# Turning the up projections of a SwiGLU layer round: tokens stationary, weights streamed

## The chip, the cores and the metric

The kernel runs on one core of one Trainium2 chip. The metric is the time of one execution on the device in microseconds (us). The profile is that of one execution; engines are named as in it: PE (matrix products), PEld (its loads of the stationary operand), DVE, ACT, POOL, and SP, which here only issues transfers.

## What is computed

One layer of a conditioned decoder trunk on 256 tokens of width 2048, all in float32: a gated feed forward, a mixer (attention heads beside a state-space part), and a second gated feed forward, each with its own shift, scale and gate from a conditioning vector and a layer norm behind it. The change touches the two feed forwards:

```python
D_MODEL = 2048
SEQ = 256
D_FF = 5632

def _modulate(h, shift, scale):
    return h * (1 + scale[:, None, :]) + shift[:, None, :]

def _swiglu(u, w1, w3, w2):
    return (jax.nn.silu(u @ w1) * (u @ w3)) @ w2

mod = (silu(c) @ w_cond[i] + b_cond[i]).reshape(B, N_SUBLAYERS, 3, D_MODEL)
u = _modulate(x, mod[:, 0, 0], mod[:, 0, 1])
h = _swiglu(u, ffn1_w1[i], ffn1_w3[i], ffn1_w2[i])
x = _layer_norm(DEEPNORM_ALPHA * x + FFN_RES_WEIGHT * (1 + mod[:, 0, 2])[:, None, :] * h, ...)
```

## The kernel before

All weights come as a stream of pieces of 128 x 1024 float32 (512 KB). A `Job` (line 110) holds one piece's source, its products (`mm`), and what is issued behind it (`post`). `Stream.run` (line 660) issues the jobs in order. For every piece SP loads `raw`, ACT rounds it to `hi` (fp32r, line 647), and DVE makes `lo = raw - hi` (line 657); activations are held as such a pair too. One product then takes three: hi with hi, hi with the activation's low part, lo with the activation's high part. `AHEAD = 4` (line 34) pieces are split ahead of PE; `RAW` and `RW` (lines 33, 59) set how many are being loaded, three or four.

The order on each engine is that of the program text. `stream.later(n, f)` puts `f` behind the n-th following piece; a post step stands on its engine ahead of the split of the piece four further on. The calls of DVE and PE pass through wrappers, and so the profile shows line 106 for all of them; ACT's own lines are kept.

**Up, before.** `form_a` (line 710) and the products in `mk_ko` (line 883) have the weights stationary, 128 x 128 at a time, and stream 256 tokens of `U`, the modulated input with its columns on the partitions (`Uh`, `Ul`). What comes out has the feed forward's columns on the partitions, as the down projection needs it. `up_post` (line 931) takes Silu on ACT (`sg`), multiplies on DVE (`h`), and splits the product into `Hh` (ACT, line 943) and `Hl` (DVE), one step per following piece.

**Down.** `mk_down` (line 960) uses `form_b` (line 731): 128 tokens of `H` stationary, 512 columns of weights streamed, both halves of the tokens one after the other, two tiles of k per piece, 12 products a piece.

**Order of a feed forward** (`ffn`, line 879). It has 44 tiles of 128 columns, treated as `PIECES` of 16, 16 and 12 tiles: up, then down, for each. The first 20 tiles are done in passes over ranges of k, because `U` gets ready bit by bit: four passes of four k-tiles in the first feed forward, two of eight in the second. Partial sums of 16 tiles go to `kosum` (copied by ACT in the first pass, added by DVE in later ones); four tiles (`KEEP`) stay in four of the eight PSUM banks. A feed forward has 264 pieces, 176 up and 88 down.

**Beside it.** Conditioning: 288 pieces of `w_cond` are loaded into `gv` and multiplied and summed by DVE (`gv_step`, line 215); a quarter of a shift and scale takes 16 of them, and `modulate` (line 280) then makes `U`. In the first feed forward's passes each piece has its share of these steps (`GA`, line 46). Afterwards `drain` (line 322) deals out conditioning steps and the preparation of the state-space matrices (`bg5`): it issues as long as DVE's estimated time is under PE's plus `LIM[0]` = 2.6. `Meter` (line 83) adds up both estimates, here for PE:

```python
n = x.shape[-1]
self.t += n / 2350.0 if name == "matmul" and a[1].dtype == F32R else max(n, 100) / 1170.0
```

Before the second feed forward the normalised rows are transposed in pairs of tiles (`turn`, line 835). Two of these steps stand in `mid` and are issued between the products of the first piece, ahead of its k-tiles 2 and 4 (`between`, line 705); the mixer's start does the same. The residual and the norm close each part (`last_block`, line 739).

Of the kernel before, what the change touches and what calls it, by code (L numbers as in the profile page):

```python
# [63 lines left out]
class Later:  # L64
    """Records the calls of an engine with their approximate costs, to be issued one by one."""
# [17 lines left out]
class Meter:  # L83
    """Passes the calls of an engine on and adds up their approximate costs in microseconds."""
# [6 lines left out]
    def __getattr__(self, name):  # L91
        f = getattr(self.engine, name)

        def call(*a, **k):
            x = k["out"] if "out" in k else a[0]
            if name in ("matmul", "transpose"):
                n = x.shape[-1]
                self.t += n / 2350.0 if name == "matmul" and a[1].dtype == F32R else max(n, 100) / 1170.0
            else:
                if name in ("tensor_reduce", "bn_stats"):  # L100
                    x = a[1]
                n = 1
                for d in x.shape[1:]:
                    n *= d
                self.t += 0.07 + n / (1920.0 if name in self.FAST else 960.0)
            return f(*a, **k)  # L106
        return call


class Job:  # L110
    """One piece of weights [128, 1024] and what is done with it."""
# [6 lines left out]
def tile_layer(tc, A, out):  # L118
    nc = tc.nc
    V, S, PE, SP, GP = Meter(nc.vector), nc.scalar, Meter(nc.tensor), nc.sync, nc.gpsimd  # L120
    with ExitStack() as ctx:
# [23 lines left out]
        def cells(t):  # L145
            """[128, 32] pieces of a slab"""
# [48 lines left out]
        # a unit is a quarter of the columns of a shift and of its scale ("p"), or half of a gate's ("g")  # L195
# [35 lines left out]
        def finish(u, acc, j0, j1):  # L231
            """gain and offset of some tiles of columns from the two halves of their sums"""
# [47 lines left out]
        def modulate(blk, q, j0=0, j1=4):  # L280
            """the second operand of the products, for some of a quarter of the columns"""
# [40 lines left out]
        def drain():  # L322
            """issues background work as VectorE has room for it"""
# [83 lines left out]
        def cmul(V, ore, oim, ar, ai, br, bi, t1, t2, conj_im=False):  # L407
            """o = a*b; with conj_im, ai and oim hold the negated imaginary parts."""
# [11 lines left out]
        def s5_prep():  # L420
# [31 lines left out]
            # powers 1 to 4 of the discretised state matrix, in the place of what is no longer used  # L452
# [15 lines left out]
            # per quarter of the groups: [inputs 512 | temporaries 256 | -c_im 128 | . | W 1024 | C 1024 | est 1024]  # L468
# [22 lines left out]
            def quarter_ops(q):  # L491
                g0 = 8 * q

                def go():
# [7 lines left out]
                    def powers(z, x, p, s0, s1):  # L502
                        """z[r] = x * p, for several powers; s0 and s1 follow from the sign of the imaginary part"""
# [201 lines left out]
        def between(k):  # L705
            """what is due before the products of k-tile k"""
            if k in mid:
                mid.pop(k)()

        def form_a(p, hi, lo, UH, UL, k0, first, last):  # L710
            """p [128 columns, 256 tokens] += weights^T u^T, eight k-tiles"""
# [7 lines left out]
        def form_b1(p, hi, lo, AH, AL, k0, t, first, last, c0=0, c1=512):  # L719
            """p [128 tokens, columns c0 to c1] += a weights, two k-tiles"""  # L720
# [18 lines left out]
        def last_block(B, ops, db, sub):  # L739
            """the last block of columns of a sub-layer: its last pieces go to one half of the tokens first"""  # L740
# [28 lines left out]
        def newton(o, sd, hv, q):  # L769
            """o = 1 / sqrt(v) from sd, its root, and hv = -v / 2"""  # L770
# [8 lines left out]
        def residual(t, db, p, c0=0, c1=512):  # L779
            """r = gate * p + z on one block of columns, and its statistics"""  # L780
# [8 lines left out]
        def ln_token(sub, t):  # L789
            """statistics and normalisation of one half of the tokens"""  # L790
# [36 lines left out]
        def load_affine(sub, new, h):  # L827
            """half of the columns of a norm's gain and bias"""
# [6 lines left out]
        def turn(ks, then):  # L835
            """pairs of column tiles of the normalised rows, transposed; what comes of each goes to then"""
# [23 lines left out]
        def affine(t, q, last):  # L860
            """x = normalised * g + b, in place"""
# [17 lines left out]
        def ffn(w13, w2, blk, passes, tiles, kept):  # L879
# [3 lines left out]
            def mk_ko(i, f, m):  # L883
                """a range of k for one tile of columns; both products at once when m is None"""
                k0, k1 = passes[i]
                keep = f in kept
                first = i == 0 or not keep
                last = i == len(passes) - 1 or not keep
                n = k1 - k0

                def mm(hi, lo):
                    ms = (0, 1) if m is None else (m,)
                    if first and ms[0] == 0:
                        B["ko", f] = psum()
                    for a, x in enumerate(ms):
                        p = B["ko", f][:, x * 256:(x + 1) * 256]
                        for k in range(n):
                            between(k0 + k)
                            w = hi[:, (a * n + k) * 128:(a * n + k + 1) * 128]
                            PE.matmul(p, w, kx(st["U"][0], k0 + k), start=first and k == 0 and x == 0, stop=False,  # L900
                                      skip_group_check=True)
                            PE.matmul(p, w, kx(st["U"][1], k0 + k), start=False, stop=False, skip_group_check=True)
                    for a, x in enumerate(ms):
                        p = B["ko", f][:, x * 256:(x + 1) * 256]
                        for k in range(n):
                            PE.matmul(p, lo[:, (a * n + k) * 128:(a * n + k + 1) * 128], kx(st["U"][0], k0 + k),
                                      start=False, stop=last and k == n - 1, skip_group_check=True)

                def post():
                    if keep:  # L910
                        if i == len(passes) - 1 and f < 16:
                            up_post(B["ko", f], f)
                        return
                    p = B["ko", f]
                    n = [x for x in range(tiles) if x not in kept].index(f)
                    if i == 0 and n % 4 == 0:
                        B["sum", n // 4] = pslab("kosum") if n // 4 < 2 else slab("kosum")
                    a = B["sum", n // 4][:, n % 4 * 512:(n % 4 + 1) * 512]
                    if i == 0:
                        S.copy(a, p)  # L920
                    else:
                        V.tensor_tensor(a, p, a, op=ALU.add)
                    if i == len(passes) - 1:
                        stream.later(1, lambda: up_post(a, f))
                if m is None:
                    src = w13[f, :, :, k0 * 128:k1 * 128].rearrange("m p x -> p m x")
                else:
                    src = w13[f, m, :, k0 * 128:k1 * 128]
                return Job(mm, src, post if m != 0 else None)

            def up_post(p, slot):
                if slot == 0:
                    st["H"] = pairs("H")
                s, h = w1([128, T], "sg"), w1([128, T], "h")
                hh, hl = kx(st["H"][0], slot), kx(st["H"][1], slot)
                S.activation(s, p[:, 0:256], AF.Silu)  # L936

                def mul():
                    V.tensor_tensor(h, s, p[:, 256:512], op=ALU.mult)
                    stream.later(1, hi)  # L940

                def hi():
                    S.copy(hh, h)  # L943
                    stream.later(1, lo)

                def lo():
                    V.tensor_tensor(hl, h, hh.bitcast(F32), op=ALU.subtract)
                stream.later(1, mul)

            def mk_up(ft, m, h, slot):  # L950
                def mm(hi, lo):
                    if m == 0 and h == 0:
                        B["ps"] = psum()
                    form_a(B["ps"][:, m * 256:(m + 1) * 256], hi, lo, *st["U"], 8 * h, h == 0, h == 1)

                def post():
                    up_post(B["ps"], slot)
                return Job(mm, halves(w13[ft, m], h), post if m and h else None)

            def mk_down(pi, db, c, nch, f):  # L960
# [17 lines left out]
                src = halves(w2[db, f // 4], f // 2 % 2)  # L978
# [6 lines left out]
            def load_z(db):  # L985
                """the gate and, for the first of the two, the input on a block of columns"""
# [31 lines left out]
            for i, (k0, k1) in enumerate(passes):  # L1018
                n = len(jobs)
                for f in range(tiles):  # L1020
                    jobs += [mk_ko(i, f, m) for m in ((None,) if k1 - k0 == 4 else (0, 1))]
                jobs[n].pre.append(lambda k0=k0, k1=k1: [gv_until("ready", blk, q) for q in range(k0 // 4, k1 // 4)])
            for pi, (f0, nf) in enumerate(PIECES):
                n = len(jobs)
                for s in range(max(0, min(tiles - f0, nf)), nf):
                    for m in range(2):
                        for h in range(2):
                            jobs.append(mk_up(f0 + s, m, h, s))
                if pi == 1:
                    for s in range(tiles - f0):  # L1030
# [554 lines left out]
```

## Time and profile before

| | |
|---|---|
| median of three runs | 1949.61 us (1946.49 to 1951.14) |
| span of the profiled execution | 1946.0 us; it has no other time of its own, and the three runs lie 0.5 to 5.1 us above it |
| mean granted clock of PE | 0.994 |
| first feed forward, passes over k | 33 to 272 us |
| its remainder | 272 to 810 us |
| mixer | 810 to 1179 us |
| second feed forward, passes over k | 1179 to 1412 us |
| its remainder | 1412 to 1946 us |

The stages are cut where PE's timeline passes from one kind of products to the next. A product's duration in the profile contains its way through the array, and products overlap; what a product costs in a stream is the step from its start to that of the next. "Busy" time of PE is the time in which any product is under way. In the views by stretches a product that lies across an edge is counted on both sides.

### The profile page before, as it was taken

The page shows a single profiled execution, that of the slowest core. Times are in us where ns is not written, and L with a number is a line of the kernel's source. Part 1 is how long each engine was busy: PE and PEld are TensorE (multiplying, and loading weights), DVE is VectorE, ACT ScalarE, POOL GpSimd, SP SyncE. Part 2 cuts the span into 40 slices and gives each one's busy share as a digit, 9 for nine tenths or more (in the row PEclk, how much of TensorE's full clock was granted, in tenths as well). Part 3 has the DMA queues.
Part 4 walks back from the last instruction along what each step waited for, and adds up shares of the span by engine and source line. Part 5 has one row for each costly group of instructions (what it writes and reads, how often), then busy time and mean ns, then how long its engine had stood idle before and what let it go on. Part 6 is the DMA issues. An engine that isn't in the chain of part 4 may idle for free.

```text
span 1946.0 us, 33739 instructions
## 1 busy us (share of the span) xinstructions
PE 1883.6 (97%) x13342; PEld 1763.9 (91%) x13342; DVE 1499.4 (77%) x2373; ACT 896.2 (46%) x1289; POOL 64.5 (3%) x119
## 2 busy tenths in 40 slices
PE   3999999999999999899999999999999999999997
PEld 2999997999889998799998888999988999899986
DVE  5899889787877888897998997888866544544468
ACT  2544544545445443443447635444444444334442
POOL 0000000000000000101210000000000000000000
PEclk9999999999999999999999999999999999999999
DMA  8999757899898889799988796998876555555573
GB/s 300 364 358 337 237 197 282 293 335 317 303 338 301 308 301 330 253 341 309 310 282 316 263 328 233 331 333 268 288 283 247 185 185 183 194 191 179 185 246 121
DMA packets 162064, 532.88 MB, mean 274 GB/s; under 512 B 21825, under 2 KB 23281, under 8 KB 160753
## 3 DMA queue, kind: packets, MB, share of 16 engines
q1 hardware_dynamic: 147330, 495.31, 72.3%
q0 software_dynamic: 6512, 23.89, 3.6%
q10 hardware_dynamic: 8064, 11.54, 1.7%
q8 instruction: 104, 1.70, 0.4%
q14 instruction: 54, 0.44, 0.1%
HBM read 513.34 MB, written 17.33 MB: 273 GB/s over the span
## 4 chain that ended last, share of the span: by engine, by line
PE 89%; DVE 6%; DMA 3%; ACT 1%; issue 1%; POOL 0%; SPq 0%; DVEq 0%; ACTq 0%; POOLq 0%
PE ps L106 89%; DVE lo L106 2%; DVE Y L106 1%; DMA gv<-in_w_cond_dram 1%; DVE gv L106 1%; DVE cells L106 1%; DMA raw<-in_f1w_dram 1%; DMA U<-sD 1%; DMA X<-in_x_dram 0%; DVE st L106 0%; ACT hi L647 0%; DVE r L106 0%; DMA sD<-sT 0%; ACT Y L818 0%; DMA sc<-in_c_dram 0%
## 5 line engine op out<-in xcount | busy, mean ns | idle before, releaser
L106 DVE TENSOR_TENSOR lo<-raw,hi 128x1024 fp32r<-128x1024 f32 x630 | 767.7, 1223 | 366.4 <-ACT hi L647 360.2
L647 ACT CAST hi<-raw 128x1024 fp32r<-128x1024 f32 x630 | 659.2, 1050 | 610.9 <-PE ps L106 422.3
L106 PE MATMUL ps<-Uh,hi 128*128 128x256 f32 x3200 | 793.4, 285 | 29.8 <-ACT hi L647 21.0
L106 PE MATMUL ps<-Ul,hi 128*128 128x256 f32 x3200 | 789.7, 284 | 0.3
L106 PEld LDWEIGHTS ps<-Uh,hi 128*128 128x128 f32 x3200 | 616.6, 193 | 37.3 <-ACT hi L647 23.0
L106 PEld LDWEIGHTS ps<-Ul,hi 128*128 128x128 f32 x3200 | 616.6, 193 | 2.2 <-DVE Ul L106 1.9
L106 PE MATMUL ps<-Uh,lo 128*128 128x256 f32 x3200 | 449.9, 283 | 0.0
L106 PEld LDWEIGHTS ps<-Uh,lo 128*128 128x128 f32 x3200 | 413.6, 192 | 0.0
L106 DVE SCALAR_TENSOR_TENSOR gv<-gv,sc 128x1024 f32<-128x1024 f32 x288 | 351.0, 1220 | 16.0 <-DMA gv<-in_w_cond_dram 8.9
L106 PE MATMUL ps<-hi,Hh 128*128 128x512 f32 (+1 forms) x716 | 274.4, 384 | 0.0
L106 PE MATMUL ps<-hi,Hl 128*128 128x512 f32 (+1 forms) x716 | 274.1, 384 | 0.0
L106 PE MATMUL ps<-lo,Hh 128*128 128x512 f32 (+1 forms) x716 | 217.6, 385 | 5.7 <-DVE lo L106 5.5
L106 PEld LDWEIGHTS ps<-lo,Hh 128*128 128x128 f32 x716 | 133.0, 189 | 34.4 <-DVE lo L106 8.2
L106 PEld LDWEIGHTS ps<-hi,Hh 128*128 128x128 f32 x716 | 134.8, 188 | 26.7 <-issue 0.4
L106 PEld LDWEIGHTS ps<-hi,Hl 128*128 128x128 f32 x716 | 134.9, 188 | 26.4
L936 ACT ACTIVATE sg<-ps 128x256 f32<-128x256 f32 x56 | 21.5, 384 | 116.0 <-PE ps L106 116.0
L106 DVE TENSOR_TENSOR kosum<-ps,kosum 128x512 f32<-128x512 f32 x64 | 44.2, 690 | 23.1 <-PE ps L106 23.1
L943 ACT CAST Hh<-h 128x256 fp32r<-128x256 f32 x88 | 35.4, 402 | 43.1 <-DVE h L106 43.0
L106 PE MATMUL ps<-hi,Ah 128*128 128x512 f32 (+1 forms) x144 | 52.1, 367 | 0.0
L106 PE MATMUL ps<-hi,Al 128*128 128x512 f32 (+1 forms) x144 | 52.0, 366 | 0.0
L106 PE MATMUL ps<-lo,Ah 128*128 128x512 f32 (+1 forms) x144 | 40.9, 366 | 0.0
L920 ACT COPY kosum<-ps 128x512 f32<-128x512 f32 x32 | 18.8, 586 | 45.2 <-PE ps L106 45.1
(211 smaller groups left out, 1182.4 us busy)
## 6 DMA issues: line engine op xcount, KB each, us to landing
gv<-in_w_cond_dram SPq DMA_DIRECT2D x288, 512.0 KB, 6.7
raw<-in_f1w_dram SPq DMA_DIRECT2D x264, 512.0 KB, 5.6
raw<-in_f2w_dram SPq DMA_DIRECT2D x264, 512.0 KB, 4.4
raw<-in_win_a_dram SPq DMA_DIRECT2D x48, 512.0 KB, 5.6
raw<-in_wout_dram SPq DMA_DIRECT2D x32, 512.0 KB, 5.5
s5m<-scrB POOLq DMA_DIRECT2D x8, 1024.0 KB, 7.9
raw<-in_win_v_dram SPq DMA_DIRECT2D x16, 512.0 KB, 4.5
scrB<-s5f ACTq DMA_DIRECT2D x8, 640.0 KB, 9.4
```

Of the source, the lines that this page charges most:

```text
L106: return f(*a, **k)
L647: S.copy(hi, raw)
L920: S.copy(a, p)
L936: S.activation(s, p[:, 0:256], AF.Silu)
L943: S.copy(hh, h)
```

## The change

The up projections take the form of the down projections. `form_b` is used in `mk_ko` and `mk_up` with `U` stationary, and w1 or w3 streamed 512 columns wide. One block is four tiles of columns; its w1 products (m = 0) come first, then those of w3 (m = 1), eight pieces each, or as many as the pass has. Only the first block of a feed forward takes w1 and w3 by turns. The result has tokens on the partitions, in two PSUM banks of 512 columns for each of w1 and w3. `gated` takes Silu behind the last w1 piece, `up_post` multiplies in place behind the last w3 piece, and two and three pieces later four 128 x 128 transposes each bring two tiles into `H`'s layout in one PSUM bank, from which ACT and DVE make `Hh` and `Hl`. The number and size of pieces stay. The weights are laid out by `blocks`, so that a piece is 128 rows of 1024 words in one run; in the first feed forward's passes it was two runs of 512 words per row.

The estimate of PE's time per product changes with it, and at the second feed forward's start the two turns come behind pieces 0 and 1, not between the first piece's products.

```diff
-                self.t += n / 2350.0 if name == "matmul" and a[1].dtype == F32R else max(n, 100) / 1170.0
+                self.t += (n + 32) / 2400.0 if name == "matmul" and a[1].dtype == F32R else max(n, 100) / 1170.0
...
-            def mk_ko(i, f, m):
+            def mk_ko(i, b, m, kp):
...
                 def mm(hi, lo):
...
+                    if first and 2 * kp == k0:
+                        B["ko", b, m] = [psum(), psum()]
+                    form_b(B["ko", b, m], hi, lo, *st["U"], 2 * kp, first and 2 * kp == k0, last and 2 * kp + 2 == k1)
...
+                    a = [B["sum", b][:, (2 * m + t) * 512:(2 * m + t + 1) * 512] for t in range(2)]
+                    for t in range(2):
+                        if i == 0:
+                            S.copy(a[t], ps[t])
+                        else:
+                            V.tensor_tensor(a[t], ps[t], a[t], op=ALU.add)
                     if i == len(passes) - 1:
-                        stream.later(1, lambda: up_post(a, f))
...
+                        if m == 0:
+                            B["a", b] = a
+                            stream.later(1, lambda: gated(a, a))
+                        else:
+                            s = B.pop(("a", b))
+                            stream.later(1, lambda: up_post(s, a, 4 * b))
+                return Job(mm, halves(w13[b, m, kp // 2], kp % 2), post if 2 * kp + 2 == k1 else None)
+
+            def gated(ps, s=None):
+                s = s or [w2([128, 512], "sg") for _ in range(2)]
+                for t in range(2):
+                    S.activation(s[t], ps[t], AF.Silu)
+                return s
+
+            def up_post(s, ps, slot):
                 if slot == 0:
                     st["H"] = pairs("H")
...
+                for t in range(2):
+                    V.tensor_tensor(s[t], s[t], ps[t], op=ALU.mult)
+
+                def turned(i):
+                    p = psum()
+                    for j in range(2):
+                        for t in range(2):
+                            PE.transpose(p[:, j * T + t * 128:j * T + t * 128 + 128],
+                                         s[t][:, (2 * i + j) * 128:(2 * i + j + 1) * 128], ident)
+                    hh, hl = (kx(x, slot + 2 * i, 0, 2 * T) for x in st["H"])
+                    S.copy(hh, p)
+                    V.tensor_tensor(hl, p, hh.bitcast(F32), op=ALU.subtract)
+                stream.later(2, lambda: turned(0))
+                stream.later(3, lambda: turned(1))
+
+            def mk_up(b, m, kp, slot):
                 def mm(hi, lo):
...
+                    if kp == 0:
+                        B["ps", m] = [psum(), psum()]
+                    form_b(B["ps", m], hi, lo, *st["U"], 2 * kp, kp == 0, kp == 7)
                 def post():
...
+                    if m == 0:
+                        B["s"] = gated(B.pop(("ps", 0)))
+                    else:
+                        up_post(B.pop("s"), B.pop(("ps", 1)), slot)
...
-                for f in range(tiles):
-                    jobs += [mk_ko(i, f, m) for m in ((None,) if k1 - k0 == 4 else (0, 1))]
+                for b in range(tiles // 4):
+                    kps = range(k0 // 2, k1 // 2)
+                    if (i, b) == (0, 0):
+                        jobs += [mk_ko(i, b, m, kp) for kp in kps for m in range(2)]
+                    else:
+                        jobs += [mk_ko(i, b, m, kp) for m in range(2) for kp in kps]
...
-        mid[2] = lambda: turn((2,), turn_mod(6))
-        mid[4] = lambda: turn((3,), turn_mod(6))
+        stream.later(0, lambda: turn((2,), turn_mod(6)))
+        stream.later(1, lambda: turn((3,), turn_mod(6)))
...
-        o[f"f{i}w13"] = np.stack(up, 1).reshape(NF, 2, 128, D)
+        o[f"f{i}w13"] = np.stack([blocks(a[f"ffn{i}_w{j}"][0]) for j in (1, 3)], 1)
```

## What the change was predicted to do

> **What bounds the kernel now.** I read the page first: the share of each engine, then the chain of work that ended last.
>
> ```profile
> PE 1883.6 (97%) x13342; PEld 1763.9 (91%) x13342; DVE 1499.4 (77%) x2373; ACT 896.2 (46%) x1289; POOL 64.5 (3%) x119
> ...
> PE 89%; DVE 6%; DMA 3%; ACT 1%; issue 1%; POOL 0%; SPq 0%; DVEq 0%; ACTq 0%; POOLq 0%
> PE ps L106 89%; DVE lo L106 2%; DVE Y L106 1%; DMA gv<-in_w_cond_dram 1%; DVE gv L106 1%; DVE cells L106 1%; DMA raw<-in_f1w_dram 1%; DMA U<-sD 1%; DMA X<-in_x_dram 0%; DVE st L106 0%; ACT hi L647 0%; DVE r L106 0%; DMA sD<-sT 0%; ACT Y L818 0%; DMA sc<-in_c_dram 0%
> ```
>
> Nine tenths of the chain are products on PE. An average can hide stages with another limit, so next come busy times by stretches of 50 us (columns: stretch, then PE, PEld, DVE, ACT, POOL, granted clock, DMA share, GB/s).
>
> ```profile
> 50.00:100.00 50.00, 50.00 (x419) 50.00 (x418) 43.82 (x79) 27.87 (x38) 0.00 (x0) 1.00 1.00 368
> 100.00:150.00 50.00, 50.00 (x419) 50.00 (x418) 48.68 (x67) 18.60 (x18) 0.00 (x0) 1.00 0.97 352
> ...
> 300.00:350.00 50.00, 49.28 (x215) 39.77 (x214) 48.92 (x110) 20.78 (x22) 0.00 (x0) 1.00 0.83 299
> ...
> 1550.00:1600.00 50.00, 50.00 (x419) 50.00 (x418) 25.06 (x27) 21.20 (x28) 0.00 (x0) 1.00 0.52 179
> ```
>
> PE has work all the time, at the full granted clock, in all four. But in the first feed forward DVE (48.68 of 50) and the DMA engines (1.00) are nearly full beside it, while in the second DVE and DMA are half idle. So the second will pay out what PE saves, and the first only as far as DVE and DMA can follow.
>
> **What one piece of weights costs PE.** Both forms run in this kernel already: the up projections stream 256 tokens, the down projections 512 columns. PE's timeline in order of time gives the true step from start to start:
>
> ```profile
> 1450.67 0.39 PE L106 MATMUL ps<-hi,Hh 128*128 128x512 f32 x1
> ...
> 1464.28 0.39 PE L106 MATMUL ps<-hi,Hh 128*128 128x512 f32 x1
> ...
> 1560.04 0.28 PE L106 MATMUL ps<-Uh,hi 128*128 128x256 f32 x1
> ...
> 1562.92 0.28 PE L106 MATMUL ps<-Uh,hi 128*128 128x256 f32 x1
> ```
>
> The second pair is one piece: 24 products in 2.88 us, 0.120 each. Between the first pair lie 60 products: 13.61 us, 0.2268 each. Twice the columns cost less than twice the time: the two rows give about 0.013 us per product and 0.107 per 256 columns. A turned piece is 12 products of 512: 2.722 us, so **0.158 us less per piece**.
>
> The DMA issues count the pieces:
>
> ```profile
> raw<-in_f1w_dram SPq DMA_DIRECT2D x264, 512.0 KB, 5.6
> raw<-in_f2w_dram SPq DMA_DIRECT2D x264, 512.0 KB, 4.4
> ```
>
> Each feed forward has 264, of which 88 go down (44 tiles in twos, four blocks); 176 go up, 352 in both. 352 x 0.158 = **55.6 us saved on PE**. The operands are as in the down form (stationary fp32r activations, moving fp32r weights), so I take its step.
>
> **What is added on PE.** Per block of 512 columns the gated product is transposed in two groups of four; 11 blocks in each of two feed forwards make 44 groups, 176 transposes. The S5 preparation shows eight inside a stream of products:
>
> ```profile
> 631.74 1.12 PE L106 MATMUL ps<-Uh,lo 128*128 128x256 f32 x8
> 632.70 1.04 PE L106 MATMUL ps<-ident,s5w 128*128 128x128 f32 x8
> 633.66 0.67 PE L106 MATMUL ps<-s5f,s5w 128*32 128x128 f32 x16
> ...
> L106 PE MATMUL ps<-ident,s5w 128*128 128x128 f32 x64 | 8.3, 272 | 0.0
> ```
>
> From the first to what follows them: 0.96 us for eight, 0.12 each, though one lasts 272 ns: they overlap. 44 x 0.48 = **21.1 us added**. The Trainium skill, "TensorE: Matmul & The Clock Gate", Part 4: PE-mode transpose, has a transpose at about 275 ns in one kernel's context; if that were the step, 176 would cost an estimated 48 us and eat nearly the whole saving. The trace agrees with it as a duration (272), not as a step.
>
> Net: 55.6 - 21.1 = 34.5 us, half in each feed forward.
>
> **What is added off PE.** Per four tiles, four multiplications and four subtractions of 256 become two and two of 512, four Silu and four casts on ACT two and two.
>
> ```profile
> L106 DVE TENSOR_TENSOR kosum<-ps,kosum 128x512 f32<-128x512 f32 x64 | 44.2, 690 | 23.1 <-PE ps L106 23.1
> L106 DVE TENSOR_TENSOR Hl<-h,Hh 128x256 fp32r<-128x256 f32 x88 | 36.8, 420 | 0.0
> ```
>
> On DVE 8 x 0.42 = 3.36 us become 4 x 0.69 = 2.76: lighter. I give it nothing, since DVE isn't the end where it has room. The order gets tighter, though. The copy of the turned block (ACT) now waits for PE's transposes, the subtraction (DVE) for that copy; behind them queue the split of the piece four ahead (hi, then lo) and, on SP, the load that follows that lo. From PE's product to the subtraction go 0.48 for the transposes and about 0.6 for the copy: DVE may stand about 1.1 us, 44 times. Cover: three pieces are split ahead, 3 x 2.72 = 8.2 us. Without it, at most 44 x 1.1 = 48 us. In the passes over k, PSUM is emptied two banks at a time with four to rotate: DVE must be done two pieces (5.4 us) after a pair, where it had three; also covered unless DVE lags by over 4 us. SP issues the same number of pieces of the same size.
>
> **The first feed forward's passes.** DVE there does lo, a conditioning step and a sum per piece:
>
> ```profile
> 104.60 0.68 DVE L106 TENSOR_TENSOR kosum<-ps,kosum 128x512 f32<-128x512 f32 x1
> ...
> 117.85 0.69 DVE L106 TENSOR_TENSOR kosum<-ps,kosum 128x512 f32<-128x512 f32 x1
> ...
> 151.22 0.17 DVE L106 SCALAR_TENSOR_TENSOR gs<-acc 128x4 f32<-128x4 f32 x1
> ...
> 155.65 1.23 DVE L106 TENSOR_TENSOR lo<-raw,hi 128x1024 fp32r<-128x1024 f32 x1 [0.53 <-ACT hi L647]
> ```
>
> Five pieces took DVE 13.25 us with no idle between. PE needs 5 x 2.88 = 14.4 now and 5 x 2.722 = 13.6 then: DVE still fits, by 0.36 us instead of 1.15. But each new quarter of k holds DVE 4.4 us with its modulation (151.22 to 155.65), and at 0.36 per five pieces it hardly catches up in the twenty of a pass. I take 1 us lost, between 0 and 40 pieces x 0.158 = 6.3.
>
> **Its remainder.** There the background (S5 preparation, conditioning) is dealt out by the program's estimate of PE's time. That estimate was 24 x 256/2350 = 2.614 us per piece, under the true 2.88; it becomes 12 x 544/2400 = 2.720, the true time. So DVE may be given 0.106 us more per piece and has no hidden margin left. 184 pieces lie here: at most 19.5 us. Where DVE was full, PE did stop:
>
> ```profile
> 300.00:320.00 20.00, 19.23 (x62) 1.00 0.75 271
> 320.00:340.00 20.00, 19.73 (x35) 1.00 0.89 326
> ...
> 420.00:440.00 20.00, 19.93 (x30) 1.00 0.88 299
> ...
> 500.00:520.00 20.00, 19.68 (x29) 1.00 0.75 267
> ...
> 766.38 1.22 PE L106 MATMUL ps<-lo,Hh 128*128 128x512 f32 x2 [2.77 <-DVE lo L106]
> ```
>
> (The middle rows are DVE's busy time in stretches of 20 us.) Some 50 pieces lie in such full stretches: 50 x 0.106 = 5.3. I take **5 us lost**, between 0 and 19.5.
>
> **The starts.** Before the second feed forward the first piece needed all of k 0 to 7, with two turns in its middle:
>
> ```profile
> 1179.02 0.58 PE L106 MATMUL ps<-Uh,hi 128*128 128x256 f32 x1 [0.91 <-DVE Uh L106]
> ...
> 1185.93 0.28 PE L106 MATMUL ps<-Uh,hi 128*128 128x256 f32 x1
> ...
> 1180.00:1200.00 20.00, 19.78 (x150) 0.94 0.65 212
> ```
>
> 6.91 us for 2.88 of work. The new first piece needs k 0 and 1 alone, and the turns come behind pieces 0 and 1: their eight transposes, and on ACT and DVE the modulation of two k each, still ahead of the splits of pieces 4 and 5, and wanted only by pieces 4 and 6. 6.91 - 2.88 - 0.96 (the transposes stay) = 3.1 at most; the granted clock of 0.94 over 20 us (the last row) is 1.2 us that stays too. I take **2 gained**, between 0 and 3.1. At the very start the opposite:
>
> ```profile
> 39.90 0.58 PE L106 MATMUL ps<-Uh,hi 128*128 128x256 f32 x1 [5.17 <-ACT Uh L293]
> ...
> 40.23 4.62 DVE L106 TENSOR_TENSOR lo<-raw,hi 128x1024 fp32r<-128x1024 f32 x4
> ```
>
> The first piece can now begin earlier with k 0 and 1, but its fifth product is of lo, which DVE makes last, at about 41.4, where the old piece went on at 39.90 with hi. I take 0.5 lost, between 0 and 1.5.
>
> **Sum.** -55.6 + 21.1 + 1 + 5 - 2 + 0.5 = -30.0 us. The span is 1946.0, to 1916.0; the median of the runs is 1949.61, 3.6 above it, and I keep that distance: **1919.6 us**.
>
> **Rivals.**
> *DVE becomes the end throughout the first feed forward.* For: 48.68 and 48.92 of 50. Against, after the passes:
>
> ```profile
> 272.30:810.40 538.10, 532.71 (x3592) 487.41 (x3591) 450.36 (x797) 248.10 (x370) 17.98 (x33) 1.00 0.85 303
> ```
>
> DVE is busy 450 of 538 us, 84%, and at most 19.5 us more could be dealt out early. The first half then gives nothing: 17.2 + 2 - 0.5 = 18.7 saved, 1930.9. Chance 0.16.
>
> *DMA.* Between 60 and 100 us:
>
> ```profile
> raw<-in_f1w_dram SPq DMA_DIRECT2D x14, 512.0 KB, 7.5
> gv<-in_w_cond_dram SPq DMA_DIRECT2D x14, 512.0 KB, 7.5
> xT<-in_xT_dram SPq DMA_DIRECT2D x1, 512.0 KB, 8.4
> ```
>
> 29 pieces in 40 us. The new pace asks 40/2.722 x 1.9 + 1 = 28.9: just what was moved. If it can't be held, the 60 + 40 pieces of the passes that share the queue with conditioning gain nothing: 15.8 less, 1935.4. Chance 0.05.
>
> *The transposes don't overlap,* at 272 ns each: 47.9 instead of 21.1, 1946.4, no change. For: groups of four lie between two waits. Against: the 0.96. Chance 0.02.
>
> *The width saves nothing:* 512 columns of these weights at twice 0.120; the point is 0.2268 + 30/(352 x 12) = 0.234. All 55.6 gone: 1975.2. Against: 60 products in a row. Chance 0.02. The Trainium skill, same page, section Back-to-back issue gap, has the gap at N/2.4 + 2.5 ns, which is 109 and 216: it would save an estimated 11 us before the transposes, and the change would lose. The measured 120 and 227 speak against that rule.
>
> *Slower, by PE's wait at the turns* of the first feed forward: a full DVE delivers the product late, and PE, which runs in order, stands at the transposes. Two pieces (5.4 us) cover it; it decides above 30/22 = 1.4 us per turn. At the 2.77 us that PE waited for a late lo, 22 x 2.77 = 61: 1980.6. Chance 0.03.
>
> **Chances and range.** The forecast, 1911 to 1926, has 0.66; better than that 0.06 (no loss in the first feed forward is 1913.6; a cheaper turn goes below). 1908 to 1935 leaves out about 0.03 below and 0.14 above. A change under 0.2% (3.9 us) can't be told from none. Faster 0.93, same 0.02, slower 0.05.
>
> **What would show it.** In the changed profile: 12 products per up piece at 0.227; eleven blocks x 2 with groups of four transposes whose next product starts 0.48 later; in the second feed forward PE without idle and about 19 us shorter; in the first, DVE near full between 100 and 350 us and a few waits of PE for lo. Wrong would be a PE idle at transposes (the turn's rival), passes that still take 2.88 per piece, or a step above 0.23.

## The result, and the profile after

The changed kernel takes 1925.01 us (median of four runs, 1920.76 to 1926.62); the kernel before, timed with it, 1948.05 (1946.22 to 1951.14). The ratio is 0.9877, with a 95% interval of 0.986 to 0.9894: 23 us faster, where 30 were forecast. The profiled execution took 1923.86 us with a span of 1921.6.

The page of the changed kernel, its span, its engines and its chain by engine:

```profile
span 1921.6 us, 25394 instructions
...
PE 1853.3 (96%) x9294; PEld 1559.2 (81%) x9294; DVE 1492.8 (78%) x2285; ACT 884.1 (46%) x1201; POOL 65.5 (3%) x119
...
PE 83%; DVE 9%; DMA 4%; ACT 2%; issue 2%; POOL 0%; SPq 0%; DVEq 0%; ACTq 0%
```

PE is busy 30 us less, DVE and ACT hardly changed. PE is still the bound, but its part of the chain falls from 89% to 83% and DVE's rises from 6% to 9%.

Where the time went is read by stages. The edges are the first product of a stage on PE's timeline: passes of the first feed forward, its remainder, mixer, the first two pieces of the second feed forward, and its rest. Before:

```profile
33.09:272.34 239.25, 234.08 (x1921) 233.61 (x1922) 208.33 (x323) 114.83 (x151) 4.01 (x4) 1.00 0.86 309
272.34:810.48 538.14, 532.75 (x3593) 487.45 (x3592) 450.36 (x797) 248.14 (x370) 18.06 (x33) 1.00 0.85 303
810.48:1179.02 368.54, 356.55 (x2485) 328.88 (x2483) 328.66 (x587) 193.69 (x354) 37.67 (x68) 0.99 0.87 301
1179.02:1188.81 9.79, 9.57 (x57) 8.52 (x57) 8.81 (x16) 8.28 (x14) 0.00 (x0) 0.83 0.27 92
1188.81:1946.00 757.19, 743.45 (x5288) 702.95 (x5286) 485.52 (x612) 323.62 (x391) 3.20 (x6) 0.99 0.66 231
```

After (columns as in the prediction: stretch, length, PE, PEld, DVE, ACT, POOL, granted clock, DMA share, GB/s; the last row is a detail of the second):

```profile
32.03:264.63 232.60, 225.87 (x992) 184.21 (x993) 206.40 (x306) 109.94 (x133) 4.02 (x4) 1.00 0.88 319
264.63:796.27 531.64, 525.15 (x2497) 432.64 (x2496) 448.13 (x770) 247.48 (x343) 19.25 (x34) 1.00 0.87 306
796.27:1166.14 369.87, 357.54 (x2485) 329.85 (x2484) 327.80 (x587) 193.37 (x354) 37.44 (x67) 0.99 0.88 300
1166.14:1181.30 15.16, 11.23 (x33) 7.80 (x33) 8.87 (x13) 6.90 (x11) 0.00 (x0) 0.66 0.26 83
1181.30:1921.60 740.30, 726.33 (x3289) 602.20 (x3287) 484.60 (x570) 318.77 (x350) 3.20 (x6) 0.99 0.69 236
640.00:660.00 20.00, 16.31 (x69) 13.04 (x68) 19.56 (x25) 6.75 (x8) 2.25 (x3) 0.91 0.83 273
```

| Stage | gain forecast | gain measured |
|---|---|---|
| first feed forward, to the end of its passes | 80 x 0.158 - 8 x 0.48 - 1 - 0.5 = 7.3 | 272.34 - 264.63 = 7.7 |
| its remainder | 96 x 0.158 - 14 x 0.48 - 5 = 3.5 | 6.5 |
| mixer | 0 | -1.3 |
| second feed forward, two pieces | 2 | -5.4 |
| its rest | 176 x 0.158 - 22 x 0.48 = 17.2 | 16.9 |
| sum | 30.0 | 24.4 |

The rows are differences between two single profiles. They agree with the prices of a piece and of a turn where PE is the bound. One row goes clearly against the forecast, the start of the second feed forward: its two pieces took 9.79 us and now take 15.16, at a granted clock of 0.66. The mixer's 1.3 us can't be put down to the change: in the other profiles below the mixer takes between 368.3 and 375.4 us, 373.7 in one that has the old form.

What PE waited for, summed over the changed kernel (us in total, times, longest):

```profile
PE ps L106 <- ACT hi L647: 21.7, 2, 19.2
PE ps L106 <- DVE lo L106: 10.8, 6, 6.6
...
PE ps L106 <- DVE sg L106: 3.7, 2, 3.4
```

Three entries matter. A second wait for `hi` (21.7 - 19.2 = 2.5 us; before there was one alone, 21.0 us at the very start) stands at the second feed forward's start. Waits for `lo` come partly from the very start (6.6), partly from the first feed forward's remainder, and 1.44 from the second feed forward's start. A wait for `sg`, the gated product, is the wait at a turn that the last rival named; it came at one turn (3.42 us, and 0.27 within the same group of transposes), not at 22.

A turn on PE's timeline, as the prediction wanted to see it:

```profile
1384.28 0.62 PE L106 MATMUL ps<-lo,Uh 128*128 128x512 f32 x2
1384.74 0.60 PE L106 MATMUL ps<-ident,kosum 128*128 128x128 f32 x4
1385.09 0.48 PE L106 MATMUL ps<-hi,Uh 128*128 128x512 f32 x1
1385.41 0.39 PE L106 MATMUL ps<-hi,Ul 128*128 128x512 f32 x1
```

Between the starts of the first and the last row lie two products, four transposes and one product, 1.13 us. Three products are 3 x 0.227 = 0.68, so the turn costs about 0.45, against 0.48.

The failed stage on all engines' timeline, at the start of the second feed forward:

```profile
1166.14 0.50 PE L106 MATMUL ps<-hi,Uh 128*128 128x512 f32 x1 [0.91 <-DVE Uh L106]
...
1169.51 1.22 PE L106 MATMUL ps<-lo,Uh 128*128 128x512 f32 x2 [1.44 <-DVE lo L106]
...
1173.09 0.88 PE L106 MATMUL ps<-ident,Y 128*128 128x128 f32 x4
...
1174.01 1.02 ACT L696 ACTIVATE uf<-ps,bt,gs 128x256 f32<-128x256 f32 x2 [6.15 <-PE ps L106]
...
1175.37 3.88 ACT L647 CAST hi<-raw 128x1024 fp32r<-128x1024 f32 x4
...
1176.46 0.50 PE L106 MATMUL ps<-hi,Uh 128*128 128x512 f32 x1 [2.49 <-ACT hi L647]
```

Read it from ACT. Its modulation (L696) waits 6.15 us for the turn's transposes, which PE reaches only when piece 0 is done (1173.09). The four casts `hi` of pieces 1 to 4 are queued behind that modulation, and PE then waits 2.49 us for the first of them. Before, the turns stood inside the first piece, so PE released ACT early:

```profile
1181.38 1.02 ACT L696 ACTIVATE uf<-ps,bt,gs 128x256 f32<-128x256 f32 x2 [0.63 <-PE ps L106]
...
1184.14 3.89 ACT L647 CAST hi<-raw 128x1024 fp32r<-128x1024 f32 x4
```

ACT waited 0.63 us for that turn, and its four casts began at 1184.14, while PE was still in piece 0 (piece 1 began at 1185.93, without a wait). That ACT's queue costs PE the time is so far a reading; the first experiment tests it.

### The profile page after: what moved, and what is told of

Its sections match the earlier page's. It is cut to its first block, busy times and chain, and to the rows that moved or that the text cites. A ratio compares the mean times of both kernels' runs of the same rounds, so it can differ in the third digit from the quotient of the medians.

```text
span 1921.6 us, 25394 instructions
## 1 busy us (share of the span) xinstructions
PE 1853.3 (96%) x9294; PEld 1559.2 (81%) x9294; DVE 1492.8 (78%) x2285; ACT 884.1 (46%) x1201; POOL 65.5 (3%) x119
## 4 chain that ended last, share of the span: by engine, by line
PE 83%; DVE 9%; DMA 4%; ACT 2%; issue 2%; POOL 0%; SPq 0%; DVEq 0%; ACTq 0%
PE ps L106 83%; DVE lo L106 3%; DVE gv L106 3%; DMA raw<-in_f1w_dram 2%; DVE Y L106 1%; DMA gv<-in_w_cond_dram 1%; DVE cells L106 1%; ACT hi L647 1%; DMA scrB<-tabr 1%; DMA U<-sD 0%; DVE kosum L106 0%; ACT uf L696 0%; DMA raw<-in_f2w_dram 0%; ACT Y L818 0%; DVE st L106 0%
## 5 line engine op out<-in xcount | busy, mean ns | idle before, releaser
L106 PE MATMUL ps<-hi,Uh 128*128 128x512 f32 x1472 | 582.0, 395 | 22.7 <-ACT hi L647 21.7
L106 PE MATMUL ps<-hi,Ul 128*128 128x512 f32 x1472 | 576.4, 392 | 0.0
L106 PE MATMUL ps<-lo,Uh 128*128 128x512 f32 x1472 | 457.0, 392 | 8.0 <-DVE lo L106 8.0
L106 PEld LDWEIGHTS ps<-hi,Uh 128*128 128x128 f32 x1472 | 278.0, 189 | 84.3 <-ACT hi L647 24.0
L106 PEld LDWEIGHTS ps<-hi,Ul 128*128 128x128 f32 x1472 | 278.3, 189 | 56.7 <-DVE Ul L106 0.5
L106 PE MATMUL ps<-Uh,hi 128*128 128x256 f32 x384 | 98.6, 293 | 2.9 <-ACT sT L1076 1.8
L106 PE MATMUL ps<-Ul,hi 128*128 128x256 f32 x384 | 96.4, 288 | 0.2
L106 PEld LDWEIGHTS ps<-Uh,hi 128*128 128x128 f32 x384 | 74.8, 195 | 6.5 <-ACT sT L1076 2.7
L106 PEld LDWEIGHTS ps<-Ul,hi 128*128 128x128 f32 x384 | 74.9, 195 | 1.1 <-DVE Ul L106 1.0
L942 ACT CAST Hh<-ps 128x512 fp32r<-128x512 f32 x44 | 25.8, 587 | 87.6 <-PE ps L106 87.6
L106 DVE TENSOR_TENSOR Hl<-ps,Hh 128x512 fp32r<-128x512 f32 x44 | 30.2, 687 | 32.8 <-ACT Hh L942 32.8
L106 PE MATMUL ps<-Uh,lo 128*128 128x256 f32 x384 | 53.9, 283 | 0.0
## 6 DMA issues: line engine op xcount, KB each, us to landing
scrB<-s5f ACTq DMA_DIRECT2D x8, 640.0 KB, 10.6
```

Of the source, the lines that this page charges most:

```text
L942: S.copy(hh, p)
```

## The experiments

Differences are against the changed kernel. It was run again beside the first three experiments: 1925.07 us, ratio 0.9877 (0.9863 to 0.989). Beside the others no changed kernel ran; there 0.9877 of their kernel before (1948.47 and 1947.93) stands for it, 1924.5 and 1924.0.

> The changed kernel once more, as the measure for the runs beside it: ratio to the kernel before 0.988, some 23 us faster.

### The turn behind the splits

```diff
-        stream.later(0, lambda: turn((2,), turn_mod(6)))
-        stream.later(1, lambda: turn((3,), turn_mod(6)))
+        stream.q[stream.done].bg.append(lambda: turn((2,), turn_mod(6)))
+        stream.q[stream.done + 1].bg.append(lambda: turn((3,), turn_mod(6)))
```

The same turns, but `bg` of a job is issued after the splits that follow the piece, `later(0)` before them.

> Only edit to the changed kernel: at the second feed forward's start the two moved turns are issued behind the split of pieces 1 to 4 (and of piece 5), not ahead of it. Theory (the order on ACT): ACT's modulation of the turned block waits for PE to finish piece 0, and the hi of pieces 1 to 4 queues behind it; with the order changed piece 1 starts without PE's 2.5 us wait and the start of piece 2, 15.2 us after the first product, comes at about 10; 4 to 6 us less in all. Rival (the slow clock and the late lo of piece 0 make the start slow): the wait before piece 1 goes but nothing else, at most 2.5 us less. Second rival (the modulation now comes too late for piece 4): the time is only moved, 0 to 1 us.

Measured: 1922.45 us (1920.35 to 1924.82), ratio 0.9862 (0.9849 to 0.9876). The totals' intervals overlap with the changed kernel's and decide nothing. Its timeline does, on the stage itself:

```profile
1170.66 0.80 PE L106 MATMUL ps<-hi,Uh 128*128 128x512 f32 x1 [0.56 <-DVE Uh L106]
...
1172.43 2.93 ACT L647 CAST hi<-raw 128x1024 fp32r<-128x1024 f32 x3
...
1174.18 1.22 PE L106 MATMUL ps<-lo,Uh 128*128 128x512 f32 x2 [1.41 <-DVE lo L106]
...
1177.76 1.05 PE L106 MATMUL ps<-ident,Y 128*128 128x128 f32 x4
...
1178.47 0.62 PE L106 MATMUL ps<-hi,Uh 128*128 128x512 f32 x1
...
1181.80 0.48 PE L106 MATMUL ps<-hi,Uh 128*128 128x512 f32 x1
```

ACT now makes `hi` of the next pieces at 1172.43, before the transposes of 1177.76, and piece 1 follows them without a wait. Two pieces take 1181.80 - 1170.66 = 11.1 us instead of 15.2. The whole second feed forward, from first product to end of span, is 1922.0 - 1170.66 = 751.3 us. In the profiles of the changed kernel, its repeat, the old estimate and the later turn it is 755.1 to 756.0, in the four kernels below and here that have this edit 750.8 to 751.7: on average 4.4 us less, with no overlap. For these 4.4 us the cause is shown. The total shows less: in this profile the stages up to the mixer took 3 us more than in the repeat and the mixer 3.5, though the edit touches neither. Of the 3.5, the wait for the transfer `U<-sD` has 1.4 (3.2 us against 1.8), and the granted clock behind that wait, 0.50 for 6.8 us instead of 3.4, has 1.7.

### The old estimate of PE's time

```diff
-                self.t += (n + 32) / 2400.0 if name == "matmul" and a[1].dtype == F32R else max(n, 100) / 1170.0
+                self.t += n / 2350.0 if name == "matmul" and a[1].dtype == F32R else max(n, 100) / 1170.0
```

> Only edit to the changed kernel: the program's estimate of PE's time is the old one again (2.614 us per piece, not 2.720). Theory of the prediction (the higher estimate hands DVE too much in the first feed forward's remainder, 5 us of PE): PE's waits for lo and for the turned product between 264 and 796 us, 6.5 us in the changed kernel, shrink to about 1, and the time falls by 3 to 5 us. Rival (the estimate only moves background work to and fro; what is held back must be issued at the end of the feed forward, where the kernel before waited 4.7 us): within 2 us of the changed kernel, with the waits at the end, after 740 us.

Measured: 1915.59 us (1912.32 to 1920.97), ratio 0.9832 (0.9816 to 0.9848): 9.5 us less, nearly twice the 5 that I had put on this term. The first feed forward's remainder, and the 20 us in which the changed kernel stood:

```profile
264.30:787.50 523.20, 522.41 (x2497) 431.74 (x2495) 448.81 (x770) 247.28 (x343) 17.59 (x34) 1.00 0.87 311
640.00:660.00 20.00, 20.00 (x92) 16.58 (x91) 17.24 (x37) 9.06 (x11) 1.50 (x2) 1.00 0.98 379
```

523.20 us instead of 532.00 in the repeat of the changed kernel. DVE's busy time is the same (448.81 and 448.38): no work went away, it lies elsewhere. The changed kernel's timeline shows what it met there:

```profile
304.57 0.73 PE L106 MATMUL ps<-lo,Hh 128*128 128x512 f32 x2 [0.59 <-DVE lo L106]
...
311.19 0.73 PE L106 MATMUL ps<-lo,Hh 128*128 128x512 f32 x2 [0.77 <-DVE lo L106]
...
315.21 0.73 PE L106 MATMUL ps<-lo,Hh 128*128 128x512 f32 x2 [1.00 <-DVE lo L106]
...
639.85 1.22 DVE L106 TENSOR_TENSOR tabc<-tabc,cells 128x1024 f32<-128x1024 f32 x1
...
640.99 1.22 DVE L106 TENSOR_TENSOR lo<-raw,hi 128x1024 fp32r<-128x1024 f32 x1
...
642.13 1.22 DVE L106 SCALAR_TENSOR_TENSOR gv<-gv,sc 128x1024 f32<-128x1024 f32 x1
...
643.27 1.28 DVE L106 TENSOR_TENSOR sg<-sg,ps 128x512 f32<-128x512 f32 x2
...
644.01 0.33 PE L106 MATMUL ps<-ident,sg 128*128 128x128 f32 x1 [3.42 <-DVE sg L106]
```

Three steps of DVE, of which one builds a table of the state-space part (`tabc`) and one is conditioning, stand ahead of the multiplication; PE waits 3.42 us at the turn. Behind the wait the clock drops (0.91 over the 20 us). With the old estimate the same tables come later (the first table step at 612 us instead of 585), this wait doesn't occur, and of the early waits for `lo` 0.79 us is left. PE's waits in the remainder fall from 6.5 to 0.79 us: they account for about 5.7 of the 8.8 us, the clock for 0.09 x 20 = 1.8; some 1.3 us I can't assign.

### Each transpose twice

```diff
-                    for j in range(2):
+                    for j in (0, 1, 0, 1):
```

In `turned`: each group of four is done two times, 176 transposes more.

> Only edit to the changed kernel: each group of four transposes is done twice, into the same places, so that 176 more transposes run in 44 groups. Theory (a transpose costs PE its step, 0.11 to 0.12 us): 19 to 21 us slower. Rival (each costs its whole duration of 0.27 us): 48 us slower. Rival (a turn costs by its waits, not by its products): under 10 us slower.

Measured: 1943.26 us (1941.78 to 1947.44), ratio 0.9969 (0.9958 to 0.998): 18.2 us more, 18.2 / 176 = 0.103 each, a little under the 19 to 21 us expected. The doubled group on its timeline:

```profile
1372.27 1.03 PE L106 MATMUL ps<-ident,kosum 128*128 128x128 f32 x8
1373.06 0.48 PE L106 MATMUL ps<-hi,Uh 128*128 128x512 f32 x1
```

Eight steps in 0.79 us from start to start, where four take 0.35 in the changed kernel: the four added cost 0.44, 0.11 each. At 0.272 each, as a duration would have it, it would have been 48 us.

### The same order, half the width

```diff
-                    form_b(B["ko", b, m], hi, lo, *st["U"], 2 * kp, first and 2 * kp == k0, last and 2 * kp + 2 == k1)
+                    form_up(B["ko", b, m], hi, lo, *st["U"], 2 * kp, first and 2 * kp == k0, last and 2 * kp + 2 == k1)
...
+                for w, xs in ((hi, (AH, AL)), (lo, (AH,))):
+                    for i in range(2):
+                        for x in xs:
+                            for c in (0, 256):
+                                PE.matmul(p[:, c:c + 256], kx(x, k0 + i, t * 128, t * 128 + 128),
+                                          w[:, i * 512 + c:i * 512 + c + 256],
...
```

Up projections alone: each product of 512 columns as two of 256, so 24 per piece as in the kernel before, with all else as changed.

> Only edit to the changed kernel: every up product of 512 columns is done as two of 256, same stationary operand, same banks, so an up piece has 24 products again. Theory (what the change saves is a fixed part of about 0.013 us in each product): an up piece takes 2.88 us again, 352 x 0.158 = 56 us come back, 1970 to 1981 us, the turns' 19 us slower than the kernel before. Rival (the saving comes from the order of the work or the stationary operand's being tokens, not from the width): within 10 us of the changed kernel.

Measured: 1972.69 us (1970.48 to 1974.39), ratio 1.0125 (1.0103 to 1.0146): 48.2 us more. The turned order without its width is slower than the kernel before; the whole gain is the width. By stages, against the repeat of the changed kernel, it costs 11.5 in the passes, 10.5 in the remainder and 25.8 in the second feed forward, where 0.158 per piece makes 12.6, 15.2 and 27.8. The shortfall is mostly in the remainder, where the slower pace shrinks the wait at the turn from 3.4 to 0.2 us: part of the width was paid back there.

Each product of 256 columns comes with its own load of the stationary operand, although the two of a pair use the same one. So the run shows a fixed cost near 13 ns for a product together with its load, and doesn't say which of the two has it.

The Trainium skill, "TensorE: Matmul & The Clock Gate", section Back-to-back issue gap, has the gap of an isolated product at N/2.4 + 2.5 ns. If that held in this stream, halving all up products would add 352 x 12 x 2.5 ns, an estimated 10.6 us. The measured 48.2 us is against it here.

### The turns one piece later

```diff
-                stream.later(2, lambda: turned(0))
-                stream.later(3, lambda: turned(1))
+                stream.later(3, lambda: turned(0))
+                stream.later(4, lambda: turned(1))
```

> Only edit to the changed kernel: the two turns of a block come three and four pieces behind the multiplication, not two and three. Theory (two pieces are too little cover where DVE is full: PE's 3.4 us wait at the transposes near 642 us, with the slow clock behind it): that wait goes, 3 to 5 us less. Rival (DVE is behind by all it was given, and PE then waits for lo): the wait turns up under lo, within 1.5 us of the changed kernel.

Measured: 1919.75 us (1917.36 to 1924.03), ratio 0.9854 (0.9835 to 0.9873). The interval overlaps with the changed kernel's, so it stays undecided. The profile, of its slowest run, shows the wait change its name:

```profile
642.42 0.74 PE L106 MATMUL ps<-lo,Uh 128*128 128x512 f32 x2 [0.78 <-DVE lo L106]
...
671.94 0.50 PE L106 MATMUL ps<-hi,Uh 128*128 128x512 f32 x1 [1.62 <-ACT hi L647]
```

The 3.42 us at the turn are gone, but DVE, as full as before, is now late with a `lo`, and the split after it with a `hi`. The remainder took 531.7 us in that profile, no less than the changed kernel's 531.6. The last turn of the passes now falls into it; passes and remainder together took 762.6 us, against 764.3 and 763.6 in the changed kernel and its repeat.

### Both edits, and a third

The order of the turn and the old estimate together; then, with both, the very first piece's `lo` made right behind its `hi`:

```diff
-                stream.split_to(1, False)
+                stream.split_to(1)
```

> The two edits together, turns behind the split at the second feed forward's start and the old estimate of PE's time. Theory (the two costs lie in different stages and add up, 4.6 and 9 us): 12 to 14 us less than the changed kernel, 1911 to 1914, with no wait of PE over 1 us between 264 and 785 us and none before piece 1 of the second feed forward. Rival (one pays for the other, because what one lets through waits in the mixer between them): 9 to 10 us less, as with the estimate alone.

> The two edits and a third: the lo of the very first piece is made right behind its hi, not behind the last conditioning steps of the first quarter. Theory (PE's 6.5 us wait for that lo near 40 us hides the whole first piece): piece 0 is done before k-tiles 2 and 3 are ready, 2 to 3 us less than with two edits. Rival (pieces 1 to 3 are split only behind those steps, and the first pass waits for them in any case): within 1 us.

Measured: 1909.82 us (1909.44 to 1913.74), ratio 0.9806 (0.9789 to 0.9823), and with the third edit 1909.55 us (1908.62 to 1911.55), ratio 0.9801 (0.9785 to 0.9816). The first two add up: 14.7 us under the changed kernel, where they showed 4.4 and 9.5 alone. PE's longest wait between 264 and 785 us is 0.76 us, and there is none before piece 1 of the second feed forward. The third gives nothing that can be told. Its first wait for `lo` falls from 6.4 us, but what follows is late anyway:

```profile
35.08 1.22 PE L106 MATMUL ps<-lo,Uh 128*128 128x512 f32 x2 [1.81 <-DVE lo L106]
...
39.84 0.80 PE L106 MATMUL ps<-hi,Uh 128*128 128x512 f32 x1 [0.98 <-ACT hi L647]
```

### The new estimate in the kernel before

```diff
-                self.t += n / 2350.0 if name == "matmul" and a[1].dtype == F32R else max(n, 100) / 1170.0
+                self.t += (n + 32) / 2400.0 if name == "matmul" and a[1].dtype == F32R else max(n, 100) / 1170.0
```

My theory after the second experiment was that an estimate at PE's true time always costs, since it leaves DVE no hidden margin.

> The kernel before with one edit, the new estimate of PE's time (an old-form up piece then counts 2.88 us and not 2.614, a down piece 2.720). Theory (any estimate as long as PE's true time hands DVE more than it can do beside PE in the first feed forward's remainder, in either form): 4 to 10 us slower than before, with new waits of PE for lo between 272 and 760 us. Rival (the loss needs the turned form, whose products wait on DVE at the turns): within 2 us of the kernel before.

Measured: 1947.88 us (1944.82 to 1953.09), ratio 1.0002 (0.9989 to 1.0015). The theory falls. PE's waits for `lo` in it:

```profile
PE ps L106 <- DVE lo L106: 2.7, 4, 1.0
```

In the kernel before it was 5.5 us in 4 waits, the longest 2.77. The new estimate brings the early waits in the old form too (around 300 to 320 us), but the late ones are gone, 2.77 at 766 us and 1.89 at 801. That fits with background work that is done sooner (the last table leaves at 687 us instead of 734), but it wasn't tested by itself. The remainder was 534.3 us instead of 538.1 in that profile, and the mixer 373.7 instead of 368.5. What the new estimate costs in the changed kernel is thus not the margin as such.

### A lower estimate

With the turn behind the splits, `n / 2500.0`: the background is spread still further back.

> The changed kernel with the turns behind the split and an estimate below the old one (n/2500, 2.458 us per piece). Theory (DVE needs some margin, and with the old estimate nearly all waits between 264 and 785 us were gone): nothing more to win, within 2 us of the run with the old estimate and the same order (1910). Rival (the less is dealt out early the better): 2 to 4 us less. Third (work held back piles up before the mixer): 3 to 8 us more, with PE waiting for lo after 740 us.

Measured: 1922.61 us (1920.28 to 1924.12), ratio 0.9865 (0.9846 to 0.9885): 12.8 us more than the 1909.82 with `n / 2350.0` and the same order, which was measured beside other runs. The two kept profiles lie only 7.3 us apart (spans of 1918.2 and 1910.9): 4.2 more in the remainder, 3.8 more in the mixer, 0.7 less elsewhere. So the traces account for 7.3 of the 12.8. PE's timeline and the stretch in front of the mixer:

```profile
791.96 0.95 PE L106 MATMUL ps<-ident,Y 128*128 128x128 f32 x4 [4.99 <-ACT Y L818]
```

```profile
780.00:800.00 20.00, 11.03 (x69) 9.59 (x68) 17.95 (x46) 6.92 (x13) 8.66 (x15) 0.80 0.75 247
```

The tables are now made as late as 671 to 787 us; what is pushed back meets the norm ahead of the mixer. PE waits 4.99 us there, a wait that the kernel with `n / 2350.0` doesn't have, and is busy 11.0 of 20 us, where it was 15.7 in the same stretch of that kernel. So the estimate has an end on each side: too high, DVE is full where a turn wants it; too low, work is left over at the stage's end.

## Why the prediction was right, and where it was not

The 1925.0 us lie inside the forecast's 1911 to 1926, at its slow edge.

**The width: right.** The forecast had 0.158 us per piece. In the changed kernel six products of 512 columns take 1.36 us from start to start (1372.49 to 1373.85), 0.227 each, as forecast. Halving the width again cost 48.2 us of the 55.6 that the term has, 0.137 per piece, with the missing part mainly in the remainder, where waits took its place.

**The transposes: right, a little high.** 0.48 us per group was forecast; it is 0.45 on the timeline, and four more cost 0.41 (18.2 / 44). The rival with 272 ns each falls, and so does that of a width that saves nothing.

**The rest of the second feed forward: right.** 17.2 us forecast, 16.9 measured. PE is its bound, and what PE saves is paid out.

**The second feed forward's start: the step that failed.** The prediction took "2 gained, between 0 and 3.1", with the modulation "still ahead of the splits of pieces 4 and 5, and wanted only by pieces 4 and 6". That is the state in mid-stream, with pieces split ahead. At a feed forward's start only piece 0 is split, and the steps that the modulation stands ahead of are the splits of pieces 1 to 4. I had asked who wants the moved step's result, and not who is queued behind it while it waits for PE. The stage lost 5.4 us, and issuing the turn behind the splits wins 4.4 us back. So the sign that the prediction named, a second feed forward without idle of PE and about 19 us shorter, didn't come: it is 11.5 us shorter (755.5 instead of 767.0), and PE has the waits shown above. This step alone is 7.4 us off, the whole miss in the span being 30.0 - 24.4 = 5.6. The order on ACT doesn't explain all of it: with the order changed the two pieces still take 11.1 us, PE still waits 1.41 us for the first piece's `lo`, and the granted clock over them is 0.64, so that up to 0.36 x 11.1 = 4.0 us go to the clock, against 1.7 before. The prediction charged such a late `lo` at the very start, but not here; making it earlier here wasn't tried.

**The estimate: right in sign and as a cause, the mechanism only in part.** The prediction charged 0.106 us of additional DVE work per piece in full stretches, 5 us in all, and kept 0 to 19.5 as bounds. Measured alone it is 9.5. But it isn't a toll per piece: the same estimate costs nothing in the old form, and a lower one costs 12.8 us in the new. The estimate decides where the tables' work falls, and in the changed kernel it fell ahead of a turn. That the stage still beat its forecast (6.5 us gained, not 3.5) is luck: the estimate cost more than was charged, and an item that the prediction left out made up for it. The kernel before had lost 4.7 us there to the two late waits, and 1.7 to the granted clock of 0.50 in the 3.4 us from 765.9; both went. The prediction quoted the wait of 2.77 and didn't credit its going. With 8.8 us for the estimate, as the old one gave back in this stage, and these two credited, the sum is 96 x 0.158 - 14 x 0.48 - 8.8 + 4.7 + 1.7 = 6.0, where 6.5 was measured. Why the third step of DVE falls just ahead of that turn with the one estimate and not with the other wasn't taken apart further.

**The rivals.** DVE as the bound in the whole first feed forward: no, it gave 7.7 + 6.5 = 14.2 us of 17.2. DMA: no, the passes gave 7.7 against 7.3. PE's wait at the turns, the one for a slower kernel: the mechanism exists, 3.42 us with what the clock adds, but at one turn of 22. DVE itself waits for ACT's copy, 32.8 us in all or 0.75 per turn, where the prediction had about 1.1. No stage shows that this costs anything:

```profile
L106 DVE TENSOR_TENSOR Hl<-ps,Hh 128x512 fp32r<-128x512 f32 x44 | 30.2, 687 | 32.8 <-ACT Hh L942 32.8
```

**The very start.** 0.5 us lost was forecast; the stage as a whole came out 0.4 better than its sum, and making `lo` earlier changed nothing.

The version with the turn behind the splits and the old estimate, 1909.8 us, beats both kernels.

## What to carry to other kernels

What one product costs in a stream is the step between starts, of both widths, in the same trace; from there the price of a form is a product of counts, and in the second feed forward, where PE is the bound, it held within a few per cent. A step that waits for another engine is charged for everything queued behind it on its own engine, and at the start of a stage that is other work than in mid-stream. An estimate that deals out background work is part of a kernel's form: when the form changes, the background's bursts land elsewhere, and the estimate should be tried afresh on both sides.

## What the hardware showed that was not expected

A wait on PE can cost more than its length. Behind the 3.42 us wait of the changed kernel, in stretches of 4 us:

```profile
640.00:644.00 4.00, 0.59 (x3) 0.16 (x1) 4.00 (x6) 0.51 (x1) 0.00 (x0) 1.00 0.48 170
644.00:648.00 4.00, 3.72 (x11) 2.96 (x12) 4.00 (x6) 1.53 (x2) 0.00 (x0) 0.57 0.93 301
648.00:652.00 4.00, 4.00 (x21) 3.33 (x20) 4.00 (x6) 1.54 (x2) 0.27 (x1) 1.00 0.81 264
```

The granted clock is 0.57 for the 4 us behind the wait, then full: 0.43 x 4 = 1.7 us on top of the 3.4. Cut finer, it is 0.50 from 644.59 to 648.00 us and 1.00 on both sides. The 0.6 to 1 us waits for `lo` around 300 to 320 us left it at 1.00. The Trainium skill, "TensorE: Matmul & The Clock Gate", Part 1: The HAM clock gate, has a clock that goes to half after an idle window of about 3.4 us and comes back after a busy one of that length; this row agrees.

At the second feed forward's start waits of 0.91, 1.44 and 2.49 us, each shorter, with one of 3.1 for `Y` just ahead of them, go with a clock of 0.66 over 15.16 us: 0.50 from 1166.83 to 1173.66 us, 1.00 to 1177.07, 0.50 to 1180.48. PE is busy 11.23 us there, and its 24 products and 8 transposes need about 6.3 at the full clock (24 x 0.227 + 8 x 0.11). So some 4.9 us go to the clock, more than to the waits of 1.44 and 2.49 together (3.9). No idle stretch of 3.4 us was needed for that, and the measurement decides: in the 3.41 us ahead of 1166.83 PE is busy 1.35. In the kernel before the same start lost 0.17 x 9.79 = 1.7 to the clock.

The length of the wait alone doesn't decide. The wait for `U<-sD` in the mixer is 1.75 us in the kernel before and 1.76 in the repeat of the changed kernel. Behind the first the clock stays at 1.00; behind the second it is 0.50 for 3.4 us.
